# Linear attention layer of an encoder trunk: projections dealt out between decay levels, v and r in one pass of 512 columns

## The chip, the cores and the metric

The kernel runs on one core of a Trainium2 chip. The time is that of the whole program in microseconds; of several runs the median counts. The engines are TensorE (PE; its weight loads are listed apart as PEld), VectorE (DVE), ScalarE (ACT), GpSimd (POOL) and SyncE (SP), which issues the transfers. Each works through its own list of instructions in order, and semaphores hold an instruction until what it needs is there.

## What is computed

A trunk of two layers over 512 tokens of width 1024, float32: a gated DeltaNet layer, then a gated linear attention (GLA) layer, each followed by a residual LayerNorm, a squared-ReLU MLP and another LayerNorm. The change lies in the GLA layer:

```python
proj = jnp.matmul(h, w_in)                      # 512 x 1024 by 1024 x 3104
q = heads(proj[..., :B_KW], B_DK) * (B_DK ** -0.5)      # 4 heads x 128
k = heads(proj[..., B_KW:2 * B_KW], B_DK)               # 4 heads x 128
v = heads(proj[..., 2 * B_KW:2 * B_KW + B_VW], B_DV)    # 4 heads x 256
r = proj[..., 2 * B_KW + B_VW:2 * B_KW + 2 * B_VW]      # 4 heads x 256
gate_logit = einsum(gl, gate_w2) + gate_b               # gl: two directions of rank 16
log_a = log_sigmoid(gate_logit) / 16
# one direction: S_t = diag(a_t) S_{t-1} + k_t v_t^T,  o_t = S_t^T q_t
o = o_f + o_b                                           # forward and backward
o = _rmsnorm(o, norm_g) * jax.nn.silu(r)
return jnp.matmul(o, w_out)
x = _layernorm(alpha * x + m, ln1_g, ln1_b)
```

## The kernel before

Large products are split in three: each float32 operand is cut into a high part (a cast on ACT, line 74) and a low part (a subtraction on DVE, line 75), and `mm3` (lines 93 to 95) adds high by high, high by low and low by high. A weight block comes by transfer into a buffer `wst` (three of them) and is split into a pair `wh`, `wl` (three pairs), 128 x 1024 numbers each. The activations stand transposed as `xth`, `xtl`.

The GLA layer (`gla`, line 465) goes head by head. `project` makes the two gate logits `lg`, from which ACT and DVE make the decay factors `a` (forward and backward), then q and k (48 products of 512 columns together), then v and r, each in 96 products of 256 columns into two accumulator banks. Silu of r needs another function table, which is loaded and put back. POOL multiplies the result `sr` by the norm's factor.

`mix` builds the 128 x 128 scores inside a block of tokens by doubling: seven levels s = 1, 2, 4 .. 64. In a level, DVE multiplies q (`qh`, lines 607 and 608) and k (`kh`, lines 611 and 612) half by half with running products of the decays, PE makes four score products `scp` (line 596), and DVE copies the part that the level's mask names into `sc` (line 621). Then the running products double: `SF` and `PB` on POOL (lines 628, 629), the two tiles `a` on DVE (lines 630, 631). After the levels come two sets of transposes `kdp`, six state products `stp`, and for each of four token blocks the output products `op`. `finish` normalises (a reciprocal root by ACT and DVE), multiplies by `sr` (line 686), transposes (`otp`) and splits into `oth`, `otl`.

The Python code writes head h's `mix`, then head h+1's `project`, then head h's `finish`. A scheduler in the language's tile layer then orders each engine's instructions by its own estimates; nothing in the kernel pins the order of PE. During the last head's `mix`, `out_part` makes the output product over the six 128-row parts of heads 0 to 2 (`oa`); `out_last` adds the residual through a product with the identity, the two parts of head 3 (`ob`) and the LayerNorm. Accumulator banks: `pj` 2, `ac` 4, `tp` 2.

Of the kernel before, what the change touches and what calls it, by code (L numbers as in the profile page):

```python
# [8 lines left out]
F32 = mybir.dt.float32  # L9
# [19 lines left out]
class Ctx:  # L29
# [17 lines left out]
    def exp_ln_after(self, ins):  # L47

        with self.tc.issue_after(ins.ins):
            self.nc.scalar.preload_act_table_set("natural_log_exp_and_others")  # L50

# [147 lines left out]
    def out_last(self, w, ks, lhs, z, tags, par):  # L199

        nc = self.nc
        ws = [[self.wrows(w, k * P, hf * 512) for k in ks[::2]] for hf in range(2)]
        for t in range(NT):
# [11 lines left out]
            self.xpose(t, self.xt[t])  # L215
# [235 lines left out]
class GlaConst:  # L451


    def __init__(self, c, pool, gate_b, norm_g, tmp):
        nc = c.nc
        self.masks = sel_masks(c, pool, tmp)
        self.gb = pool.tile([P, 2, B_H], F32, name="gb", bufs=1)
        nc.gpsimd.dma_start(self.gb, gate_b.rearrange("n (h p) -> p n h", p=P), allow_slow_non_contiguous=True)
        self.ngb = pool.tile([P, 2, B_H], F32, name="ngb", bufs=1)
        nc.gpsimd.tensor_scalar(self.ngb, self.gb, -1.0, None, ALU.mult)  # L460
        self.gbc = pool.tile([P, B_DV], F32, name="gbc", bufs=1)
        nc.gpsimd.dma_start(self.gbc, norm_g.partition_broadcast(P))


def gla(c, gc, w_in, gate_w2, w_out, ln_g, ln_b):
    tc, nc = c.tc, c.nc
    H = B_H
    with c.banks(pj=2, ac=4, tp=2), tc.tile_pool(name="gla", bufs=2) as pool:
# [26 lines left out]
        g = (glh, gll, w2h, w2l, gc.gb, gc.ngb, gc.gbc)  # L495
# [15 lines left out]

def gla_vr(c, pool, w_in, c0, name):

    parts = []
    for q in range(2):
        st = c.wst.tile([P, 4, B_DV], F32, name="wst", tag="wst")
        c.dma(st, w_in[q * 512:(q + 1) * 512, c0:c0 + B_DV].rearrange("(k p) n -> p k n", p=P))
        parts.append(c.split(st, [P, 4, B_DV]))
    out = []
    for tp in range(2):  # L520
        ps = c.bank([P, 2, B_DV], F32, name=name, tag="pj")
        for ti in range(2):
            sl = slice((2 * tp + ti) * P, (2 * tp + ti + 1) * P)
            for k in range(KT):
                wh, wl = parts[k // 4]
                c.mm3(ps[:, ti, :], c.xth[:, k, sl], c.xtl[:, k, sl], wh[:, k % 4, :], wl[:, k % 4, :],
                      k == 0, k == KT - 1)
        out.append(ps)
    return out


class GlaHead:


    def __init__(self, c, pool, h, w_in, gates, masks, oth, otl):
        self.c, self.pool, self.h, self.w_in = c, pool, h, w_in
        self.gates, self.masks, self.oth, self.otl = gates, masks, oth, otl
# [4 lines left out]
    def project(self, qk=None):  # L542
        c, pool, h, w_in = self.c, self.pool, self.h, self.w_in
        V, A = c.nc.vector, c.nc.scalar
        H = B_H
        glh, gll, w2h, w2l, gb, ngb, gbc = self.gates

        self.A = []
        for d in range(2):
            ps = c.bank([P, S], F32, name="lg", tag="ac")  # L550
            rows = slice(32 * d, 32 * d + 16)
            c.mm3(ps, w2h[rows, h * P:(h + 1) * P], w2l[rows, h * P:(h + 1) * P], glh[rows, :], gll[rows, :], True, True)
            e = self.t2("ge", 1)
            A.activation(e, ps, AF.Abs, bias=gb[:, d, h:h + 1])
            A.activation(e, e, AF.Exp, scale=-1.0)
            A.activation(e, e, AF.Ln, bias=1.0)
            r = self.t2("gr", 1)
            A.activation(r, ps, AF.Relu, bias=ngb[:, d, h:h + 1], scale=-1.0)
            V.tensor_tensor(r, r, e, ALU.add)
            a = self.t2(f"a{d}")  # L560
            A.activation(a, r, AF.Exp, scale=-1.0 / 16.0)
            self.A.append(a)
        qps = qk[0] if qk else c.proj_cm(w_in, h * P, "pj", name="pjq")
        self.q = self.t2("q")
        A.mul(self.q, qps, float(P) ** -0.5)
        kps = qk[1] if qk else c.proj_cm(w_in, H * P + h * P, "pj", name="pjk")
        self.k = self.t2("k")
        A.copy(self.k, kps)
        self.v = pool.tile([P, NT, B_DV], F32, name="v", tag="v", bufs=2)
        for i, ps in enumerate(gla_vr(c, pool, w_in, 2 * H * P + h * B_DV, "pjv")):  # L570
            A.copy(self.v[:, 2 * i:2 * i + 2, :], ps)
        self.sr = sr = pool.tile([P, NT, B_DV], F32, name="sr", tag="sr", bufs=2)
        for i, ps in enumerate(gla_vr(c, pool, w_in, 2 * H * P + H * B_DV + h * B_DV, "pjr")):
            last = A.activation(sr[:, 2 * i:2 * i + 2, :], ps, AF.Silu)
        c.exp_ln_after(last)
        c.nc.gpsimd.tensor_tensor(sr, sr, gbc.unsqueeze(1).to_broadcast([P, NT, B_DV]), ALU.mult)

    def mix(self):
        c, pool, q, k, v = self.c, self.pool, self.q, self.k, self.v
        V, A, T, G = c.nc.vector, c.nc.scalar, c.nc.tensor, c.nc.gpsimd  # L580
        t2 = self.t2

        PF, SB = self.A
        SF, PB = t2("SF", 1), t2("PB", 1)
        c.nc.gpsimd.memset(SF, 1.0)
        c.nc.gpsimd.memset(PB, 1.0)
        sc = pool.tile([P, NT, P], F32, name="sc", tag="sc", bufs=1)

        def blk(t, s):
            return t.rearrange("p (b two s) -> p b two s", two=2, s=s)  # L590

# [10 lines left out]
        k2 = t2("kh")  # L602
        A.mul(k2, k, 2.0)
        s = 1
        while s < P:
            qh = t2("qh")
            V.tensor_tensor(blk(qh, s)[:, :, 1, :], blk(q, s)[:, :, 1, :], blk(PF, s)[:, :, 1, :], ALU.mult)  # L607
            V.tensor_tensor(blk(qh, s)[:, :, 0, :], blk(q, s)[:, :, 0, :], blk(SB, s)[:, :, 0, :], ALU.mult)
            if s > 1:
                kh = t2("kh")  # L610
                V.tensor_tensor(blk(kh, s)[:, :, 0, :], blk(k, s)[:, :, 0, :], blk(SF, s)[:, :, 0, :], ALU.mult)
                V.tensor_tensor(blk(kh, s)[:, :, 1, :], blk(k, s)[:, :, 1, :], blk(PB, s)[:, :, 1, :], ALU.mult)  # L612
            else:
                kh = k
            ps = score(kh, qh)
# [6 lines left out]

            nb = S // (2 * s)

            def bc(t, half, idx):
                return blk(t, s)[:, :, half, idx:idx + 1].to_broadcast([P, nb, s])

            G.tensor_tensor(blk(SF, s)[:, :, 0, :], blk(SF, s)[:, :, 0, :], bc(PF, 1, s - 1), ALU.mult)
            G.tensor_tensor(blk(PB, s)[:, :, 1, :], blk(PB, s)[:, :, 1, :], bc(SB, 0, 0), ALU.mult)
# [623 lines left out]
```

## Time and profile before

| | us |
|---|---|
| median of 3 runs | 1469.55 |
| the runs | 1468.07 to 1469.78 |
| the profiled execution | 1473.26 |
| its span in the profile | 1471.6 |
| PE busy | 1388.9 (94%) |
| DVE busy | 1024.1 (70%) |
| ACT busy | 682.5 (46%) |
| POOL busy | 208.6 (14%) |

The GLA layer lies at about 815 to 1130 us of the span: first projections from 815.6, the heads to 1103, then the output product. The mean granted clock of PE over the span is 0.989 of full speed. A record of a product lasts longer than the step to the next one, since products overlap in the array; steps are therefore read from starts. A row of a timeline gives start, length, engine, line, operation, out<-in, shape and count, and in brackets the idle time of the engine before it and what ended it. One float32 product shows as two records, a split one (`mm3`) as one record for each of its three.

### The profile page before, as it was taken

The numbers are of one execution on the slowest core, as the hardware profiler recorded it, in microseconds if no ns is written. First come the engines' busy times: TensorE is split into PE (matmuls) and PEld (weight loads), VectorE is DVE, ScalarE is ACT, GpSimd is POOL, SyncE is SP. The second block draws the span as 40 slices with busy tenths as digits, with TensorE's granted clock in tenths as the row PEclk, the third lists the DMA queues.
The fourth block names the chain that finished last, engine by engine and source line by source line (L and its number), as shares of the span: only waits on it lengthen the run. The fifth ranks groups of instructions, "written<-read, shape, count | busy, mean of one in ns | idle before, by whom it ended". The sixth has DMA issues, their size and how long they took to land.

```text
span 1471.6 us, 21001 instructions
## 1 busy us (share of the span) xinstructions
PE 1388.9 (94%) x8333; PEld 1141.9 (78%) x8333; DVE 1024.1 (70%) x1637; ACT 682.5 (46%) x1218; POOL 208.6 (14%) x220
## 2 busy tenths in 40 slices
PE   7999999999989999999999989899799999999997
PEld 6676777677767888888887878787677888888886
DVE  6878887988677666758655465857648577767655
ACT  3766556655633545444541434344123544454530
POOL 4221331133211300000001131222202000000000
PEclk9999999999999999999999999999899999999999
DMA  6221211211132743341121412111113642332221
GB/s 175 61 58 35 53 30 44 58 44 44 44 108 65 230 126 93 99 129 45 56 91 28 117 57 58 46 56 44 43 58 106 211 138 77 115 100 58 57 72 57
DMA packets 145882, 117.24 MB, mean 80 GB/s; under 512 B 7360, under 2 KB 122168, under 8 KB 145784
## 3 DMA queue, kind: packets, MB, share of 16 engines
q1 hardware_dynamic: 143856, 111.49, 25.8%
q0 software_dynamic: 1360, 4.33, 1.0%
q8 instruction: 65, 1.06, 0.3%
q14 instruction: 34, 0.27, 0.1%
q10 hardware_dynamic: 567, 0.08, 0.0%
HBM read 113.79 MB, written 2.10 MB: 79 GB/s over the span
## 4 chain that ended last, share of the span: by engine, by line
PE 52%; issue 27%; DVE 12%; ACT 5%; POOL 3%; DMA 2%; DVEq 0%; POOLq 0%; ACTq 0%
PE pj L93 4%; PE pj L95 4%; PE pj L94 4%; PE op L1190 2%; DVE qh L607 1%; PE pX L93 1%; PE pX L95 1%; PE pX L94 1%; POOL xt L178 1%; DVE wl L75 1%; PE pl L95 1%; PE pl L93 1%; PE oa L94 1%; PE m L1168 1%; PE pl L94 1%
## 5 line engine op out<-in xcount | busy, mean ns | idle before, releaser
L75 DVE TENSOR_TENSOR wl<-wst,wh 128x1024 fp32r<-128x1024 f32 x140 | 178.2, 1276 | 195.2 <-ACT wh L74 193.6
L74 ACT CAST wh<-wst 128x1024 fp32r<-128x1024 f32 x140 | 146.9, 1049 | 270.4 <-PE pj L94 159.3
L93 PE MATMUL pj<-xth,wh 128*128 128x512 f32 (+1 forms) x544 | 202.8, 373 | 0.7 <-ACT xth L133 0.7
L95 PE MATMUL pj<-xth,wl 128*128 128x512 f32 (+1 forms) x544 | 202.4, 372 | 1.0 <-DVE wl L75 1.0
L94 PE MATMUL pj<-xtl,wh 128*128 128x512 f32 (+1 forms) x544 | 202.3, 372 | 0.1
L75 DVE TENSOR_TENSOR w2l<-w2r,w2h 128x1024 fp32r<-128x1024 f32 x84 | 102.6, 1221 | 50.3 <-ACT w2h L74 49.9
L95 PEld LDWEIGHTS pj<-xth,wl 128*128 128x128 f32 x544 | 103.1, 190 | 19.5 <-DVE wl L75 1.5
L93 PEld LDWEIGHTS pj<-xth,wh 128*128 128x128 f32 x544 | 103.1, 190 | 18.3 <-ACT xth L133 0.9
L94 PEld LDWEIGHTS pj<-xtl,wh 128*128 128x128 f32 x544 | 103.2, 190 | 18.1 <-DVE xtl L134 0.3
L74 ACT CAST w2h<-w2r 128x1024 fp32r<-128x1024 f32 x84 | 88.2, 1050 | 58.4 <-DMA w2r<-in_mlp_w 21.1
L1044 POOL TENSOR_TENSOR off<-ath,off 128x1024 f16<-128x1024 f16 x32 | 72.5, 2274 | 40.8 <-PE lv L1086 39.4
L74 ACT CAST ah<-h 128x1024 fp32r<-128x1024 f32 x40 | 42.2, 1054 | 56.2 <-DVE h L317 21.9
L178 POOL TENSOR_TENSOR xt<-xt,ln 128x512 f32<-128x512 f32 x8 | 10.6, 1320 | 383.3 <-ACT xt L177 371.6
L1039 POOL TENSOR_TENSOR atl<-on,ath 128x512 f16<-128x512 f32 x16 | 22.2, 1392 | 243.4 <-ACT ath L1038 243.1
L94 PE MATMUL pX<-w2l,ah 128*128 128x512 f32 x144 | 56.1, 389 | 0.0
L95 PE MATMUL pX<-w2h,al 128*128 128x512 f32 x144 | 56.0, 389 | 0.0
L93 PE MATMUL pX<-w2h,ah 128*128 128x512 f32 x144 | 56.0, 389 | 0.0
L75 DVE TENSOR_TENSOR al<-h,ah 128x1024 fp32r<-128x1024 f32 x40 | 48.8, 1220 | 2.8 <-ACT ah L74 1.5
L596 PE MATMUL scp<-qh,kh 128*128 128x128 f32 x192 | 27.8, 290 | 19.1 <-DVE kh L612 19.1
L144 ACT ACTIVATE rsy<-rsv 128x1 f32<-128x1 f32 (+1 forms) x28 | 5.8, 207 | 84.9 <-DVE rsv L143 84.7
L596 PEld LDWEIGHTS scp<-qh,kh 128*128 128x128 f32 x192 | 24.1, 197 | 26.5 <-issue 20.4
L93 PE MATMUL pjk<-xth,wh 128*128 128x512 f32 (+1 forms) x112 | 42.6, 380 | 0.5 <-ACT wh L74 0.5
(446 smaller groups left out, 3827.2 us busy)
## 6 DMA issues: line engine op xcount, KB each, us to landing
wst<-in_mlp_w SPq DMA_DIRECT2D x80, 512.0 KB, 4.1
w2r<-in_mlp_w SPq DMA_DIRECT2D x48, 512.0 KB, 3.7
wst<-in_a_w_in SPq DMA_DIRECT2D x32, 512.0 KB, 4.0
wst<-in_b_w_in SPq DMA_DIRECT2D x24, 512.0 KB, 3.9
wst<-in_a_w_out SPq DMA_DIRECT2D x8, 512.0 KB, 3.7
wst<-in_b_w_out SPq DMA_DIRECT2D x8, 512.0 KB, 3.9
xt<-in_x SPq DMA_DIRECT2D x4, 512.0 KB, 7.0
z<-in_x SPq DMA_DIRECT2D x8, 256.0 KB, 5.3
```

Source lines behind the costliest of these rows:

```text
L74: nc.scalar.copy(hi, src)
L75: nc.vector.tensor_tensor(lo, src, hi.bitcast(F32), ALU.subtract)
L93: mm(ps, ah, bh, start=start, stop=False, **kw)
L94: mm(ps, ah, bl, start=False, stop=False, **kw)
L95: mm(ps, al, bh, start=False, stop=stop, **kw)
L178: nc.gpsimd.tensor_tensor(out[q], out[q], par[2 + q], ALU.add)
L596: T.matmul(ps[:, n, :], kh[:, sl], qh[:, sl], start=True, stop=True)
L607: V.tensor_tensor(blk(qh, s)[:, :, 1, :], blk(q, s)[:, :, 1, :], blk(PF, s)[:, :, 1, :], ALU.mult)
L1039: G.tensor_tensor(atl[:, us, :], at, ath[:, us, :], ALU.subtract)
L1044: eng.tensor_tensor(t, ath, m.unsqueeze(1).to_broadcast([P, U, P]), ALU.mult)
L1168: T.matmul(m2, self.xf[:, d * NT + n, :], r, start=True, stop=True)
L1190: T.matmul(op[:, n, :], l, r, start=i == 0, stop=i == len(mm) - 1)
```

## The change

- `in_order`: a block in which each PE instruction is made to follow the one written before it. The GLA heads stand in such a block, so PE's order is the order of the Python code.
- A generator `stream` yields projections in pieces of six products of 512 columns: 16 pieces for a head's v and r, 8 for the next head's q and k, and after head 3, 16 pieces of `out_pieces` over the first four parts. `behind(n)` takes n pieces. They are placed between levels (4 before s = 4, then 3 before each score) and one by one between the state and output products.
- `vr` makes v and r side by side: a weight block holds two of the eight row parts with 256 columns of v and 256 of r (two transfers), and four banks, one for each token tile, gather 512 columns each.
- Forward and backward decays stand in one tile `F`, the products that POOL kept in one tile `E`. `diag` is an access pattern that takes alternate stretches of s columns from the two halves, so that `qh`, `kh` and the doubling of `F` are one DVE instruction each over 512 columns. The doubling of `E` is two DVE instructions of 256 columns; POOL keeps one memset a head.
- The scores of s = 1 and s = 2 of the next head are placed in the output products of this one, its gates behind the levels s = 16 and 32, the norm of a head behind the pieces of level s = 8 of the next.
- The norm's factor is a column `gcol`, applied where the transposed output is copied and split.
- `out_last` now covers four parts (heads 2 and 3), and three of its four weight pairs are split into the places of `v`, `sr` and `F`. Banks: `ac` 2, `tp` 2, `pj` 4.

```diff
-    with c.banks(pj=2, ac=4, tp=2), tc.tile_pool(name="gla", bufs=2) as pool:
+    with c.banks(ac=2, tp=2, pj=4), tc.tile_pool(name="gla", bufs=2) as pool:
...
-        heads[0].project(qk0)
-        for h in range(H):
-            heads[h].mix()
-            if h + 1 < H:
-                heads[h + 1].project()
-            else:
-                for hf in range(2):
-                    c.out_part(w_out, list(range(2 * h)), lhs, z, "pj", hf)
-            heads[h].finish()
+        early = list(range(KT // 2))
+        with c.in_order(mybir.EngineType.PE):
+            list(heads[0].qk(qk0))
+            heads[0].gates(0)
+            heads[0].gates(1)
+            def stream():
+                for h in range(H):
+                    yield from heads[h].vr()
+                    yield from heads[h + 1].qk() if h + 1 < H else c.out_pieces(w_out, early, lhs, z, "pj")
...
+            behind(8)
+            after = None
+            level = heads[0].levels()
+            next(level)
+            for h in range(H):
+                for s in level:
+                    behind(0 if s == 2 else 4 if s == 4 else 3)
+                    if s == 8 and after:
+                        after()
+                    if s in (16, 32) and h + 1 < H:
+                        heads[h + 1].gates(s // 32)
+                level = heads[h + 1].levels() if h + 1 < H else iter(())
+                heads[h].states(behind, level)
+                after = heads[h].norm
+            behind(2)
+            after()
+            behind(99)
         c.new_x()
-        c.out_last(w_out, [2 * H - 2, 2 * H - 1], lhs, z, ("ac",), par)
+        c.out_last(w_out, list(range(KT // 2, KT)), lhs, z, ("pj",), par,
+                   [None, (pool, "v", "sr", 2), (pool, "F", "F", 2), (pool, "v", "sr", 2)])
...
+        for q in range(KT // 2):
+            st = c.wst.tile([P, 2, 2 * B_DV], F32, name="wst", tag="wst")
+            rows = slice(2 * q * P, 2 * (q + 1) * P)
+            for i, c0 in enumerate((v0, r0)):
+                c.dma(st[:, :, i * B_DV:(i + 1) * B_DV], self.w_in[rows, c0:c0 + B_DV].rearrange("(k p) n -> p k n", p=P))
+            wh, wl = c.split(st, [P, 2, 2 * B_DV])
+            if ps is None:
+                ps = [c.bank([P, 2 * B_DV], F32, name="pjv", tag="pj") for _ in range(NT)]
+            for t in range(NT):
...
+                yield
...
-            V.tensor_tensor(blk(qh, s)[:, :, 1, :], blk(q, s)[:, :, 1, :], blk(PF, s)[:, :, 1, :], ALU.mult)
-            V.tensor_tensor(blk(qh, s)[:, :, 0, :], blk(q, s)[:, :, 0, :], blk(SB, s)[:, :, 0, :], ALU.mult)
+            V.tensor_tensor(blk(qh, s), blk(q, s), diag(F, s), ALU.mult)
             if s > 1:
                 kh = t2("kh")
-                V.tensor_tensor(blk(kh, s)[:, :, 0, :], blk(k, s)[:, :, 0, :], blk(SF, s)[:, :, 0, :], ALU.mult)
-                V.tensor_tensor(blk(kh, s)[:, :, 1, :], blk(k, s)[:, :, 1, :], blk(PB, s)[:, :, 1, :], ALU.mult)
+                V.tensor_tensor(blk(kh, s), blk(k, s), diag(E, s), ALU.mult)
...
-            G.tensor_tensor(blk(SF, s)[:, :, 0, :], blk(SF, s)[:, :, 0, :], bc(PF, 1, s - 1), ALU.mult)
-            G.tensor_tensor(blk(PB, s)[:, :, 1, :], blk(PB, s)[:, :, 1, :], bc(SB, 0, 0), ALU.mult)
-            V.tensor_tensor(blk(PF, s)[:, :, 1, :], blk(PF, s)[:, :, 1, :], bc(PF, 0, s - 1), ALU.mult)
-            V.tensor_tensor(blk(SB, s)[:, :, 0, :], blk(SB, s)[:, :, 0, :], bc(SB, 1, 0), ALU.mult)
+            for i in range(2):
+                e = blk(E[:, i, :], s)[:, :, i, :]
+                V.tensor_tensor(e, e, bc(1 - i, 1 - i, (1 - i) * (s - 1)), ALU.mult)
+            a = F[:, 0, :]
+            x = bass.AP(a.tensor, a.offset + s, [list(a.ap[0]), [2 * s, nb], [S - 1, 2], [0, s]])
+            V.tensor_tensor(diag(F, s), diag(F, s), x, ALU.mult)
+            yield s
```

How the instructions move is seen in each engine's list. First DVE inside the levels of a middle head, around the copy of level s = 16 (`mu_6389` is its mask). Before:

```order
L607 TENSOR_TENSOR qh<-q,a_9738 128x8x32
L621 COPY_PREDICATED sc<-mu_6389,scp 128x512
L608 TENSOR_TENSOR qh<-q,a_9751 128x8x32
L612 TENSOR_TENSOR kh<-k,PB 128x8x32
L630 TENSOR_TENSOR a_9738<-a_9738 128x8x32
L611 TENSOR_TENSOR kh<-k,SF 128x4x64
L631 TENSOR_TENSOR a_9751<-a_9751 128x8x32
```

Now:

```order
L703 TENSOR_TENSOR E<-E,F 128x8x32 x2
L706 TENSOR_TENSOR F<-F 128x8x2x32
L91 TENSOR_TENSOR wl<-wst,wh 128x1024
L714 COPY_PREDICATED sc<-mu_6389,scp 128x512
L689 TENSOR_TENSOR qh<-q,F 128x512
L692 TENSOR_TENSOR kh<-k,E 128x512
```

The halves have become whole instructions, the two updates that stood on POOL stand on DVE, and splits of weights lie between the levels.

Second PE, from the transposes and first scores of a middle head to its next scores. Before (between the rows shown lie further products of `pjq`):

```order
L95 MATMUL pjr<-wh,xtl 128x256
L690 MATMUL otp<-ident,o 128x128 x8
L596 MATMUL scp<-qh,k 128x128 x4
L596 MATMUL scp<-q,kh 128x128 x4
L596 MATMUL scp<-qh,kh 128x128 x4
L93 MATMUL pjq<-xth,wh 128x512
L94 MATMUL pjq<-xtl,wh 128x512
```

Now, at the same levels, from the last output product of the head before (between the rows shown lie further products of `pjv`; the first run of them is 24 long, the second 18):

```order
L766 MATMUL op<-st_9158,qd 128x256
L678 MATMUL scp<-qh,kh 128x128 x4
L109 MATMUL pjv<-wh,xth 128x512
L110 MATMUL pjv<-wl,xth 128x512
L111 MATMUL pjv<-wh,xtl 128x512
```

```order
L785 MATMUL otp<-ident,o 128x128 x8
L678 MATMUL scp<-qh,kh 128x128 x4
L109 MATMUL pjv<-wh,xth 128x512
```

The scores that stood in a row of three, with runs of about ten q and k products behind them, now have runs of 18 to 24 products of v, r, q or k between them, and the first two levels have moved up into the head before.

Third PE at the end of the last head. Before, 118 `oa` products lie between the last output product and the transposes:

```order
L673 MATMUL op<-st_10765,kh 128x256
L94 MATMUL oa<-wl,oth 128x512
L95 MATMUL oa<-wh,otl 128x512
L93 MATMUL oa<-wh,oth 128x512
```

Now it is the last `out_pieces`, the output product, and 14 `ob` products (two with the identity, twelve of `mm3`):

```order
L766 MATMUL op<-st_10446,qd 128x256
L241 MATMUL ob<-xt_5720,ident 128x512
L109 MATMUL ob<-wh,oth 128x512
L110 MATMUL ob<-wl,oth 128x512
L111 MATMUL ob<-wh,otl 128x512
```

and on ACT beside it, where `v<-wst` is the cast of the last weight block into the place of `v`:

```order
L768 COPY o<-op 128x256
L90 CAST v<-wst 128x1024
L770 ACTIVATE sq,ss<-o 128x256
L160 ACTIVATE rsy<-rsv 128x4
L161 ACTIVATE rsy<-rsy 128x4
L788 ACTIVATE oth<-otp,gcol 128x512 x2
```

The stream is used up there, so the norm of the last head has the first products of `out_last` beside it, and the cast stands ahead of the last sum of squares.

More of the change, by code (lines that the diff above doesn't have):

```diff
@@ L50, in exp_ln_after, with in_order @@
             self.nc.scalar.preload_act_table_set("natural_log_exp_and_others")
+    @contextlib.contextmanager
+    def in_order(self, engine):
+        traced = self.nc.cur_bb.bb.instructions
+        last = traced[-1]
+        yield
+        start = next(k for k in reversed(range(len(traced))) if traced[k] is last) + 1
+        prev = None
+        for i in list(traced[start:]):
+            if i.engine == engine:
+                if prev is not None:
+                    self.tc.add_manual_dep(
+                        i, prev.name, mybir.DependencyInfo(mybir.DependencyClass.NoSync, mybir.DependencyReason.DATA),
+                        reason="in_order")
+                prev = i
     @contextlib.contextmanager
@@ L539, in t2, with gates @@
     def t2(self, name, bufs=2):
         return self.pool.tile([P, S], F32, name=name, tag=name, bufs=bufs)
-    def project(self, qk=None):
-        c, pool, h, w_in = self.c, self.pool, self.h, self.w_in
+    def gates(self, d):
+        c, h = self.c, self.h
         V, A = c.nc.vector, c.nc.scalar
[L545 to L568, printed above, removed]
-        self.v = pool.tile([P, NT, B_DV], F32, name="v", tag="v", bufs=2)
[L570 to L576, printed above, removed]
@@ new lines, in gates, with qk @@
+        V.tensor_tensor(r, r, e, ALU.add)
+        A.activation(self.F[:, 1 - d, :], r, AF.Exp, scale=-1.0 / 16.0)
+    def qk(self, ps=None):
+        c, h = self.c, self.h
+        A = c.nc.scalar
+        self.q, self.k = self.t2("q"), self.t2("k")
+        for i, (t, nm) in enumerate(((self.q, "pjq"), (self.k, "pjk"))):
+            if ps is None:
+                wh, wl = c.wcols(self.w_in, (i * B_H + h) * P)
+                bk = c.bank([P, S], F32, name=nm, tag="pj")
+                for k in range(KT):
+                    c.mm3(bk, wh[:, k, :], wl[:, k, :], c.xth[:, k, :], c.xtl[:, k, :], k == 0, k == KT - 1)
+                    if k % 2:
+                        if k == KT - 1:
+                            self.keep(i, t, bk)
+                        yield
+            else:
+                self.keep(i, t, ps[i])
@@ L639, in kdec @@
             for n in range(NT):
[L640 to L641 removed]
+                T.transpose(ps[:, n, :], kd[d][:, n * P:(n + 1) * P], c.ident)
+            o = pool.tile([P, NT, P], F32, name=f"kdt{d}", tag=f"kdt{d}", bufs=1)
             A.copy(o, ps)
[L643 to L653 removed]
+            kt.append(o)
@@ L654, in mix @@
+        states = [{}, {}]
+        cur = [None, None]
+        for i in range(NT - 1):
+            for d in range(2):
+                if i < 2 and d == 0:
+                    behind(1)
+                n = i if d == 0 else NT - 1 - i
+                ps = c.bank([P, B_DV], F32, name="stp", tag=("ac", "tp")[d])
+                T.matmul(ps, kt[d][:, n, :], v[:, n, :], start=True, stop=True)
                 nw = pool.tile([P, B_DV], F32, name=f"st{d}", tag=f"st{d}", bufs=3)
-                if cur is None:
+                if cur[d] is None:
@@ L669, in mix @@
+                    V.scalar_tensor_tensor(nw, cur[d], tot, ps, ALU.mult, ALU.add)
+                states[d][n + 1 - 2 * d] = cur[d] = nw
+        self.ss = c.small.tile([P, NT], F32, name="ss", tag="ss")
+        self.ob = {}
+        for n in (1, 2, 0, 3):
+            behind(1)
+            if n != 1 and n != 3:
+                next(level, None)
             sl = slice(n * P, (n + 1) * P)
-            ops = c.bank([P, B_DV], F32, name="op", tag="ac")
+            ops = c.bank([P, B_DV], F32, name="op", tag=("ac", "tp")[n % 2])
```

169 lines of the change are left out of this document (101 added, 68 removed).

## Prediction

> **What bounds the kernel now.** I read the stage first: the busy time of each engine between the head of the linear attention layer and its output product (columns: length; busy time and instructions of PE, PEld, DVE, ACT, POOL; clock; DMA share).
>
> ```profile
> 833.00:1105.00 272.00, 246.19 (x1576) 216.96 (x1574) 174.61 (x309) 105.50 (x191) 59.00 (x66) 0.97 0.19 55
> ```
>
> TensorE (PE) is the busiest, VectorE (DVE) is at 64%, nothing else is near. Then who made PE wait there (total, times, longest):
>
> ```profile
> PE scp L596 <- DVE kh L612: 19.1, 20, 2.4
> PE pjr L94 <- DVE wl L75: 4.9, 4, 2.3
> PE stp L653 <- ACT kdt L642: 1.4, 2, 0.7
> ```
>
> The scores `scp` wait for `kh`, the last DVE product of a decay level. The PE timeline shows how one level looks, and the same score one head later (988.72):
>
> ```profile
> 929.57 0.39 PE L94 MATMUL pjq<-xtl,wh 128*128 128x512 f32 x1
> 930.90 1.16 PE L596 MATMUL scp<-qh,kh 128*128 128x128 f32 x8 [0.94 <-DVE kh L612]
> 931.81 0.47 PE L95 MATMUL pjq<-xth,wl 128*128 128x512 f32 x1
> ...
> 933.51 0.40 PE L93 MATMUL pjq<-xth,wh 128*128 128x512 f32 x1
> 934.62 1.13 PE L596 MATMUL scp<-qh,kh 128*128 128x128 f32 x8 [0.71 <-DVE kh L612]
> ...
> 988.72 1.16 PE L596 MATMUL scp<-qh,kh 128*128 128x128 f32 x8 [0.94 <-DVE kh L612]
> ```
>
> A level lasts 3.7 us (930.90 to 934.62), of which PE has 0.9 us of score and 1.9 us of `pjq`. A head lasts 57.8 us. The level is 3.7 us long because DVE and POOL go in turn:
>
> ```profile
> 878.99 0.85 DVE L607 TENSOR_TENSOR qh<-q,a 128x256 f32<-128x256 f32 x1
> ...
> 880.38 0.41 DVE L608 TENSOR_TENSOR qh<-q,a 128x256 f32<-128x256 f32 x1
> ...
> 881.37 0.85 DVE L611 TENSOR_TENSOR kh<-k,SF 128x256 f32<-128x256 f32 x1
> ...
> 882.48 0.84 DVE L607 TENSOR_TENSOR qh<-q,a 128x256 f32<-128x256 f32 x1
> ```
>
> ```profile
> 878.88 0.68 POOL L628 TENSOR_TENSOR SF<-SF,a 128x256 f32<-128x256 f32 x1 [0.76 <-DVE kh L611]
> 881.26 0.68 POOL L629 TENSOR_TENSOR PB<-PB,a 128x256 f32<-128x256 f32 x1 [1.70 <-DVE kh L612]
> ```
>
> The same 128x256 product takes 0.41 us alone and 0.85 when it starts under a POOL product. So the level sections run at the pace of DVE and PE is half filled, while v and r, 192 products a head, run in one dense block in which DVE has little to do.
>
> **What PE's work is without waits.** Rows for the step from one product to the next:
>
> ```profile
> 839.26 0.38 PE L93 MATMUL pjv<-wh,xth 128*128 128x256 f32 x1
> 839.48 0.28 PE L94 MATMUL pjv<-wl,xth 128*128 128x256 f32 x1
> 850.76 0.28 PE L95 MATMUL pjv<-wh,xtl 128*128 128x256 f32 x1
> 927.49 0.40 PE L94 MATMUL pjq<-xtl,wh 128*128 128x512 f32 x1
> 1039.77 0.60 PE L690 MATMUL otp<-ident,o 128*128 128x128 f32 x4
> 1040.21 1.06 PE L596 MATMUL scp<-qh,k 128*128 128x128 f32 x8
> 1041.10 1.06 PE L596 MATMUL scp<-q,kh 128*128 128x128 f32 x8
> 1075.48 0.59 PE L673 MATMUL op<-v,sc 128*128 128x256 f32 x2
> 1075.91 0.59 PE L673 MATMUL op<-st,kh 128*128 128x256 f32 x2
> 1104.32 1.02 PE L208 MATMUL ob<-xt,ident 128*128 128x512 f32 x2
> ```
>
> From 839.48 to 850.76 lie 94 steps of 256 columns: 0.120 us each. From 927.49 to 929.57 lie nine of 512 columns: 0.231. Eight score records take 0.89, so 0.111 each; two `op` records 0.43; four transposes 0.44. Between the first v product (839.26) and the output product (1104.32) lie 265.1 us. The work in it: v and r 768 x 0.120 = 92.2; q and k of three heads 144 x 0.231 = 33.3; `oa` 144 x 0.231 = 33.3; scores 256 x 0.111 = 28.4; `op` 80 and `stp` 48 x 0.215 = 27.5; transposes 64 x 0.11 = 7.0; gate products of three heads, 18 at 0.231 at most, 4.2. Sum 225.9, so **39 us are lost**. The waits above name 25; each is shown some 0.16 short, since a 0.39 record lasts past its 0.23 step. Most of the rest is slow clock, as behind the wait for `wl` (same columns as the first row):
>
> ```profile
> 909.00:912.00 3.00, 0.91 (x8) 0.70 (x6) 2.24 (x5) 2.21 (x2) 1.01 (x1) 1.00 0.00 0
> 912.00:915.00 3.00, 2.83 (x13) 2.83 (x14) 1.25 (x2) 0.00 (x0) 0.00 (x0) 0.52 0.55 148
> ```
>
> **The change part by part.**
>
> *The stream between levels.* Each head's 24 pieces of six 512-column products (6 x 0.231 = 1.39 us) are now dealt out: 4, then 3 per level, then one by one between the state products. A level then holds 3 x 1.39 + 0.89 = 5.1 us of PE work against DVE's. DVE per head, from the groups of the stage (count, busy, mean ns):
>
> ```profile
> L75 DVE TENSOR_TENSOR wl<-wst,wh 128x1024 fp32r<-128x1024 f32 x30 | 36.7, 1236 | 54.7 <-ACT wh L74 54.4
> L621 DVE COPY_PREDICATED sc<-mu,scp 128x512 f32<-128x512 uint8 x24 | 17.3, 720 | 0.5 <-PE scp L596 0.5
> L608 DVE TENSOR_TENSOR qh<-q,a 128x256 f32<-128x256 f32 x28 | 11.5, 412 | 1.2 <-ACT a L561 1.1
> L686 DVE SCALAR_TENSOR_TENSOR o<-o,rs,sr 128x256 f32<-128x256 f32 x16 | 8.5, 590 | 0.1
> L658 DVE SCALAR_TENSOR_TENSOR st<-st,a,stp 128x256 f32<-128x256 f32 x16 | 7.6, 477 | 4.0 <-PE stp L653 3.9
> L664 DVE TENSOR_TENSOR kh<-q,a 128x512 f32<-128x512 f32 x8 | 5.1, 680 | 0.0
> ```
>
> Six `wl` 7.4; 26 products of 512 (`qh` 7, `kh` 6, `F` 7, `kd` 2, `qd` 2, `gr` 2) at 0.68, 17.7; 14 updates of `E`, new on DVE, at 0.412, 5.8; 7 masked copies 5.0; 4 states 1.9; 4 `o` 2.4; two `otl` taken as 512-column products 1.4; the small ones of the root 0.8. Sum **42.4 us**. PE in a middle head has v and r 22.2 (below), q and k 11.1, and a quarter of the other terms, (28.4 + 27.5 + 7.0)/4 = 15.7, with gates about 50 us. So PE becomes the bound of the whole head, with DVE at 85%, and no POOL product is left to hold DVE up. For a level: 0.68 x 3 + 0.41 x 2 + 0.72 = 3.6 us and a `wl` in most, 4.8 at most against 5.1.
>
> What I walked through in the order lists for one middle head: `kh` and `qh` stand one to two levels ahead of their score; the copies `kdt` have a piece between them and `stp`; each score bank is read a piece or more before it comes round again. The tight places are the second score right behind the first eight (its bank waits for ACT's copy `sc`), and casts `wh` that stand in ACT's queue ahead of such copies. Bounds of the remaining waits: 0 to 5 us a head (today's 39 us are about 10 a head, and a cast is a quarter of that). I take 1.5 a head, near the lower end, since nothing in the walk was late: **+6** with **-39** for what goes.
>
> *v and r together.* 384 products of 512 columns instead of 768 of 256: 384 x 0.231 = 88.7, **-3.5** (0.009 us for each pair made one).
> The Trainium skill ("TensorE: Matmul & The Clock Gate", "Wait — 56ns, not 53.3ns?") puts a product's step at its columns over 2.4 GHz and about 2.5 ns. By it a pair made one saves 2.5 ns, an estimate of 1.0 us in all; the rows above differ, and I go by them. Silu and its table loads stay, four halves instead of two wholes, on ACT with 105.5 busy of 272. The multiplication of `sr` on POOL goes; the factor enters in two existing instructions.
>
> *The junction before it.*
>
> ```profile
> 815.63 0.29 PE L93 MATMUL gps<-xth,wh 128*48 128x256 f32 x1 [0.87 <-DVE xt L282]
> 819.33 0.66 PE L130 MATMUL tp<-ident,xt 128*128 128x128 f32 x4 [0.78 <-DVE xt L175]
> 820.64 0.66 PE L130 MATMUL tp<-ident,xt 128*128 128x128 f32 x4 [0.66 <-POOL xt L178]
> ```
>
> PE's list now has 30 q and k products (3.6 us) ahead of these transposes instead of 24 gate ones (2.7), and 18 behind them, where PE waited for `xth`. The first and third wait stay (they hang on the last residual add and on POOL), the second and the ones behind go, about 1.8, and a stretch of half clock that followed: **-3**, bounds 0 and -5.
>
> *The tail.* The last head's norm has nothing left in the stream. Today 118 `oa` products (27 us) stand between the last `op` and its transposes; laid bare it costs its whole chain, from the last `op` (1075.91) to the end of the four `o` products:
>
> ```profile
> 1079.64 1.67 DVE L686 SCALAR_TENSOR_TENSOR o<-o,rs,sr 128x256 f32<-128x256 f32 x4
> ```
>
> ```profile
> L74 ACT CAST wh<-wst 128x1024 fp32r<-128x1024 f32 x31 | 32.6, 1052 | 77.6 <-PE pjq L94 26.9 <-PE oa L95 20.3 <-PE pjr L95 14.9
> ```
>
> 1081.3 - 1076.2 = 5.1 us, of which some 1.2 are two additions of `oa` that won't lie there; a cast (1.05), new on ACT ahead of the last `sq`, makes it 5. PE has 14 `ob` products ahead of the transposes: two with the identity, a pair of records and about 0.9 each (1104.32), and twelve of 0.231, 4.6 us. Left open 0.4, then `oth`, the split of the last weights and `otl` one behind the other under the second identity product, about 1 more: **+1.5**, bounds 0 and +5. The upper one is the whole chain open and a half clock behind it, as the rows at 909 show one after 3 us with 0.9 us of work.
> The Trainium skill ("TensorE: Matmul & The Clock Gate", "What's actually happening") lets the clock fall after an idle window of about 3.4 us. The stretch at 909 was not idle throughout and fell all the same, so the looser reading by the row stays in the bound; by the page the upper end would be +4.
>
> **Sum**: -39 + 6 - 3.5 - 3 + 1.5 = -38. Against the profiled execution (1473.26, span 1471.6), from whose rows it is made, that is 1435.3. That execution stands 3.7 us over the median of the runs, 1469.55, so in their terms it is **1432 us** (1431.6).
>
> **Rivals.**
> *Order too stiff.* PE's order is now fixed, so whatever is late blocks all behind it. Casts (1.05 us) wait until PE has used up the block three before (the weights have three buffers), and they stand ahead of `kdt`, `sc` and `o` in ACT's queue. Four such hits a head: 4 x 4 x 1.05 = 17 instead of 6, and the tail at +5: 1432 + 11 + 3 = 1446. For it: `wl` and casts are what PE waited for at 909. Against: the old block needed two v parts at once until all v was done; now a part is free after 5.6 us.
> *Nothing left open*: no remaining wait, tail 0, junction -5: 1432 - 6 - 1.5 - 2 = 1422.
> *Slower: DVE takes over.* The 20 products a head that reach across both halves of `F` or `E` have no row before. Taken at 0.68 they leave DVE at 42.4; at (57.8 - 42.4)/20 = 0.77 more, 1.45 us each, DVE is as long as today's head, and above that the kernel is slower. At 1.7: 42.4 + 20.4 = 62.8, +5 a head, 1490 us. Against it: `L608`, whose runs go from one element in two up to 64, has mean 412 ns over all 28.
> The Trainium skill ("SBUF — State Buffer", "Door 1: The DMA port swizzle") says an access that crosses to a new 16-byte line pays; no row shows such a jump at each element. By it only the two products at s = 1 would pay, not 20.
> *It does little*: gains eaten by waits nobody sees, 1469.
>
> **How the numbers follow.** Forecast 0.68 (1423 to 1441), stiff order 0.18, nothing open 0.07, slower 0.05, little 0.02. The range 1420 to 1451 leaves out the two last cases, the worse half of the stiff one and a little below. Faster by over 0.2% (about what a measurement of this kernel can tell from no change) 0.93, same 0.02, slower 0.05.
>
> **What would show it.** Right: scores with waits under 0.3 us, next to no half clock between the heads, PE products of v and r at 0.231, DVE near 85% and POOL empty there, a head of 51 to 53 us. Wrong: two-half products over 1 us; PE waiting for ACT copies in the states; a tail gap over 5 us.

## The result, and the profile after

The changed kernel takes 1429.46 us (median of 4 runs, 1427.94 to 1431.42) against 1468.93 us for the kernel before (4 runs, the same chip): a ratio of 0.9732, 95% interval 0.9715 to 0.9749, 39.5 us faster. The forecast was 1432 us, in a range of 1420 to 1451. The profiled execution took 1431.42 us; its span is 1429.7.

First the view that carried the forecast: the busy time of each engine in a stretch of time (columns as in the prediction), for the changed kernel. The first row is the heads from their first levels to the output product, the second 50 us in the middle of them.

```profile
838.00:1050.00 212.00, 212.00 (x1082) 177.68 (x1080) 160.09 (x274) 105.86 (x196) 2.86 (x3) 1.00 0.22 68
940.00:990.00 50.00, 50.00 (x259) 41.86 (x258) 37.49 (x65) 26.51 (x50) 0.95 (x1) 1.00 0.20 64
```

PE is busy for the whole of it, at full clock, where it had 246 of 272 us at a clock of 0.97. POOL has gone from 59.0 us to 2.9. DVE is at 75%.

Second, what PE waited for, from the heads to the end of the output product's LayerNorm (total, times, longest):

```profile
PE tp L146 <- POOL xt L194: 1.8, 4, 0.6
PE otp L785 <- DVE o L781: 0.3, 1, 0.3
PE pj L110 <- DVE xtl L150: 0.3, 1, 0.3
```

All of these lie behind 1050; up to there no wait of PE is listed. The 19.1 us for `kh` and the 4.9 for `wl` are gone.

Third, PE's timeline over one head, transposes to transposes (start, length, engine, line, operation, out<-in, shape, count):

```profile
931.62 0.60 PE L736 MATMUL kdp<-ident,ge 128*128 128x128 f32 x4
...
950.94 1.05 PE L678 MATMUL scp<-qh,kh 128*128 128x128 f32 x8
...
957.33 1.05 PE L678 MATMUL scp<-qh,kh 128*128 128x128 f32 x8
...
963.19 1.06 PE L678 MATMUL scp<-qh,kh 128*128 128x128 f32 x8
...
969.17 1.16 PE L678 MATMUL scp<-qh,kh 128*128 128x128 f32 x8
...
982.66 0.60 PE L736 MATMUL kdp<-ident,ge 128*128 128x128 f32 x4
```

A head lasts 51.0 us (982.66 - 931.62) where it lasted 57.8, and no score has a bracket with a wait. The scores shown are 5.9 to 6.4 us apart (the last two of the head, 975.26 and 980.39, 5.1), longer than the 3.7 before, since a level now holds the work that stood in the dense block.

Fourth, the borders by which the gain can be put in its places, on PE:

```profile
815.68 0.39 PE L111 MATMUL pl<-w2r 128*128 128x512 f32 x1
...
836.84 0.50 PE L109 MATMUL pjv<-wh,xth 128*128 128x512 f32 x1
837.17 0.39 PE L110 MATMUL pjv<-wl,xth 128*128 128x512 f32 x1
...
840.16 0.39 PE L111 MATMUL pjv<-wh,xtl 128*128 128x512 f32 x1
...
1049.46 1.02 PE L241 MATMUL ob<-xt,ident 128*128 128x512 f32 x2
```

`pl` is the last product of the MLP ahead of the layer. In the kernel before it stands here:

```profile
814.37 0.39 PE L95 MATMUL pl<-w2r 128*128 128x512 f32 x1
```

| stretch | before | after | difference |
|---|---|---|---|
| last `pl` to first v product | 24.9 | 21.2 | -3.7 |
| first v product to output product | 265.1 | 212.6 | -52.4 |
| output product to the end of the span | 367.2 | 380.2 | +13.0 |
| last `pl` to the end | 657.2 | 614.0 | -43.2 |

48 products of `oa` (two of six parts; 48 x 0.231 = 11.1 us) have moved from the second stretch into the third. Without this move the second is -41.4 and the third +1.9. The spans differ by only 41.9, because the unchanged work ahead of `pl` took 1.3 us longer in this execution. That stretch varies: over the ten profiles of this study in which nothing ahead of `pl` was edited, the last `pl` starts at 811.6 to 815.7. So below, profiles are compared from the last `pl` to the end, and this number is called **the rest**: 657.2 before, 614.0 now.

### The profile page after: what moved, and what is told of

Its sections match the earlier page's. It is cut to its first block, busy times and chain, and to the rows that moved or that the text cites. A ratio compares the mean times of both kernels' runs of the same rounds, so it can differ in the third digit from the quotient of the medians.

```text
span 1429.7 us, 20124 instructions
## 1 busy us (share of the span) xinstructions
PE 1373.9 (96%) x7949; PEld 1117.8 (78%) x7949; DVE 1017.0 (71%) x1613; ACT 689.9 (48%) x1234; POOL 153.6 (11%) x156
## 4 chain that ended last, share of the span: by engine, by line
PE 58%; issue 28%; DVE 6%; ACT 5%; POOL 2%; DMA 1%; DVEq 0%; POOLq 0%; ACTq 0%
PE pj L110 4%; PE pj L111 4%; PE pj L109 4%; PE pjv L109 3%; PE pjv L111 2%; PE pjv L110 2%; PE scp L678 2%; PE op L1285 2%; PE pjq L111 1%; PE pjq L109 1%; PE pjq L110 1%; PE pjk L111 1%; PE pjk L110 1%; PE pjk L109 1%; PE op L766 1%
## 5 line engine op out<-in xcount | busy, mean ns | idle before, releaser
L91 DVE TENSOR_TENSOR wl<-wst,wh 128x1024 fp32r<-128x1024 f32 x137 | 175.2, 1280 | 163.8 <-ACT wh L90 162.5
L90 ACT CAST wh<-wst 128x1024 fp32r<-128x1024 f32 x137 | 143.6, 1048 | 240.3 <-PE pj L110 166.9
L111 PEld LDWEIGHTS pj<-xth,wl 128*128 128x128 f32 x544 | 102.9, 189 | 19.1 <-DVE wl L91 1.3
L109 PE MATMUL pjv<-wh,xth 128*128 128x512 f32 x128 | 54.8, 428 | 0.0
L111 PE MATMUL pjv<-wh,xtl 128*128 128x512 f32 x128 | 50.2, 392 | 0.0
L110 PE MATMUL pjv<-wl,xth 128*128 128x512 f32 x128 | 49.9, 390 | 0.0
```

The costliest lines, as they stand in the source:

```text
L90: nc.scalar.copy(hi, src)
L91: nc.vector.tensor_tensor(lo, src, hi.bitcast(F32), ALU.subtract)
L109: mm(ps, ah, bh, start=start, stop=False, **kw)
L110: mm(ps, ah, bl, start=False, stop=False, **kw)
L111: mm(ps, al, bh, start=False, stop=stop, **kw)
```

## The experiments

Two theories stood against each other. The first says that the gain comes from the order: with projections behind each score, PE has work while DVE makes the next level. The second says that it comes from the cheaper level on DVE and from the end of the turns with POOL. One more kernel sizes a single term, two look for the point at which DVE takes over, two try what the new profile suggests. No experiment changes the outputs; the extra products in two of them are written to a tile and replaced at once. The runs below were taken in three sets on three chips, each with the kernel before beside it (medians 1470.60, 1469.21 and 1470.01 us): the ratios are against these, and a difference of a microsecond between medians of two sets says little. In the diffs, line by line, - is the kernel that the edit starts from.

### v and r in 256 columns again

```diff
-                    c.mm3(ps[t], c.xth[:, k, sl], c.xtl[:, k, sl], wh[:, j, :], wl[:, j, :], k == 0, k == KT - 1)
+                    for n in range(2):
+                        cs = slice(n * B_DV, (n + 1) * B_DV)
+                        c.mm3(ps[t][:, cs], c.xth[:, k, sl], c.xtl[:, k, sl], wh[:, j, cs], wl[:, j, cs],
+                              k == 0 and n == 0, k == KT - 1, skip_group_check=True)
```

> The changed kernel with v and r again in products of 256 columns (768 instead of 384), all else kept, the order of the pieces too. By the rows before (0.120 us for 256 columns, 0.231 for 512) 768 x 0.120 - 384 x 0.231 = +3.5 us, so 1433.0 us against 1429.5. If the wide pass were worth nothing, since PE has other slack, 1429.5. If the step of a product were its columns over 2.4 GHz and 2.5 ns, +1.0: 1430.5.

It took 1433.87 us (ratio 0.9748, 0.9733 to 0.9762). Two kernels timed beside it on the same chip, which behave as the change does (next section), took 1429.50 and 1429.74, so the price is 4.1 to 4.4 us. The rest of its span is 617.9, 3.9 more. Its PE timeline has the step of a 256-column product:

```profile
842.74 0.28 PE L109 MATMUL pjv<-wh,xth 128*128 128x256 f32 x1
...
843.94 0.28 PE L110 MATMUL pjv<-wl,xth 128*128 128x256 f32 x1
```

Ten steps in 1.20 us: 0.120 each, and in the change thirteen of 512 columns from 837.17 to 840.16, 0.230 each. 384 x (0.240 - 0.230) = 3.8 us. With PE full, all of it shows in the time.

### The old level body in the new order

Once whole (the products by halves on DVE, the doubling of `E` on POOL), and once only the doubling of `E` on POOL:

```diff
-            V.tensor_tensor(blk(qh, s), blk(q, s), diag(F, s), ALU.mult)
+            for i in (1, 0):
+                V.tensor_tensor(blk(qh, s)[:, :, i, :], blk(q, s)[:, :, i, :], blk(F[:, i, :], s)[:, :, i, :], ALU.mult)
...
-                V.tensor_tensor(e, e, bc(1 - i, 1 - i, (1 - i) * (s - 1)), ALU.mult)
+                c.nc.gpsimd.tensor_tensor(e, e, bc(1 - i, 1 - i, (1 - i) * (s - 1)), ALU.mult)
```

> The changed kernel with the level body of before: products of q and k half by half, the doubling of E on POOL, that of F in two DVE instructions. Theory 1 (the gain comes from dealing the projections out between the levels, so that DVE's level time is hidden): a level of 3.7 us and a split of weights of 1.2 still fit under 5.1 to 6 us of PE, so 0 to +5: 1429 to 1435. Theory 2 (the gain comes from the cheaper level on DVE and the end of the turns with POOL): most of the gain is gone, over 1450.

> The changed kernel with the doubling of E on POOL instead of DVE, the wide products of q, k and F kept. It puts back the turns between DVE and POOL alone. Theory 1: hidden, 0 to +3, 1429 to 1433. Theory 2: a level gets 2 x 0.7 us longer, 7 x 1.4 x 4 = 39 us in the worst case, about 1460.

They took 1429.74 (0.9723, 0.9706 to 0.9739) and 1429.50 us (0.9723, 0.9706 to 0.9740), with a rest of 614.6 and 614.3: no difference from the change. The middle of the heads with the old body:

```profile
940.00:990.00 50.00, 50.00 (x259) 41.83 (x258) 37.71 (x74) 26.48 (x50) 13.46 (x15) 1.00 0.21 64
```

POOL is back with 13.5 us, DVE has as many busy microseconds as in the change (37.7 against 37.5), and PE is full all the same. The groups of DVE in that kernel's heads show that the turns with POOL are back as well:

```profile
L708 DVE TENSOR_TENSOR F<-F 128x256 f32<-128x256 f32 x56 | 31.6, 586 | 11.0 <-POOL E L705 10.9
```

DVE waits 10.9 us for POOL before these updates, and one of them takes 586 ns. PE shows of it one wait of 0.5 us for `qh`; the rest is hidden. The second theory falls for this order: here the body is worth nothing that these runs can tell.

### The stream in lumps

Everything as in the change, but v and r in one block, q and k between the levels, nothing between the state products:

```diff
-            behind(8)
+            behind(16)
...
-                    behind(0 if s == 2 else 4 if s == 4 else 3)
+                    behind({2: 0, 4: 2, 8: 2, 16: 2, 32: 1, 64: 1}[s])
...
-                heads[h].states(behind, level)
+                heads[h].states(lambda n: None, level)
+                behind(16)
```

> The changed kernel with the stream taken in lumps, as before: v and r of the next head in one block of 16 pieces behind the outputs, q and k (8 pieces) between the levels, nothing between the state products. DVE's new level body, the 512-column pass and the pinned order stay. Theory 1: levels bare again, about 3.4 us of DVE against 2.6 of PE, a head of about 55.5 instead of 51.0 us: +18, 1447, between 1440 and 1460. Theory 2: the level body carries the gain, 1429 to 1435.

It took 1449.41 us (0.9854, 0.9839 to 0.9869); the rest is 636.2, 22.1 more than in the change. Its waits of PE, over heads and output product:

```profile
PE kdp L737 <- DVE ge L726: 9.6, 4, 2.7
PE scp L679 <- DVE qh L690: 1.7, 1, 1.7
PE scp L679 <- DVE kh L693: 1.3, 1, 1.3
PE scp L679 <- ACT sc L712: 0.9, 1, 0.9
```

and the engines while the levels of a middle head run:

```profile
912.00:932.00 20.00, 18.77 (x105) 15.15 (x103) 19.09 (x32) 11.87 (x18) 0.00 (x0) 1.00 0.19 54
```

DVE is at 95% there and PE no longer full: the wait has moved from the scores to the transposes behind the last level. Half of the gain of the change is gone by the order alone, with the new body in place. The first theory's 1447 was near. The waits listed come to 13.5 of the 22.1 us. Most of the others is slow clock behind the waits, as in the last head:

```profile
1040.00:1046.00 6.00, 3.13 (x20) 2.36 (x18) 6.00 (x13) 2.09 (x2) 0.00 (x0) 0.96 0.25 87
1046.00:1052.00 6.00, 5.28 (x16) 4.25 (x17) 4.05 (x7) 1.92 (x4) 0.00 (x0) 0.50 0.15 38
```

Over the 232 us from 838 to 1070 the granted clock is 0.96, where the change has 1.00. By these two figures up to 232 x 0.04 = 9 us are lost to the clock, an estimate.

What the pin does by itself is not shown: every kernel with the stream was run with it. What this experiment changes is the order in which the pieces are written.

### The new level body in the kernel before

```diff
-            V.tensor_tensor(blk(qh, s)[:, :, 1, :], blk(q, s)[:, :, 1, :], blk(PF, s)[:, :, 1, :], ALU.mult)
-            V.tensor_tensor(blk(qh, s)[:, :, 0, :], blk(q, s)[:, :, 0, :], blk(SB, s)[:, :, 0, :], ALU.mult)
+            V.tensor_tensor(blk(qh, s), blk(q, s), diag(F, s), ALU.mult)
```

and likewise `kh`, `E` and `F` as in the change; no stream, no written order.

> The kernel before with the new level body alone (F and E in one tile each, wide products, no POOL in a level); projections, banks, norm and output product as before. The scheduler's list for it is not that of before: it now places 13 to 28 products behind each score of levels 4 to 64 where it placed about 10, since it sees cheaper levels, and v products move there too. Theory 1 (what counts is how much PE work lies behind a level): most of the waits for kh go by this order, -25 to -35, 1440. Theory 2 (the shorter level itself): 0.4 us in 24 levels, -10, 1459, with waits of 0.5 us left at the scores.

It took 1442.15 us (0.9816, 0.9798 to 0.9834), 27 us less than the kernel before. That is near the first theory's 1440. So the body that is worth nothing in the new order goes with most of the gain in the old one. Its wait for the scores:

```profile
PE scp L599 <- DVE kh L613: 4.3, 4, 1.6
```

4.3 us where the kernel before has 19.1. But this is not the body alone: with other instructions the scheduler made another list for PE, in which most scores from s = 4 on have 12 to 28 products behind them. What is left of the wait follows that list. The four waits stand at the scores of s = 4, which have none, 7, 9 and 7 products ahead of them in the four heads; no score with 12 or more ahead of it has a wait. In the second head, 7 products lie between the first two rows and 13 between the last two:

```profile
917.47 1.06 PE L599 MATMUL scp<-qh,kh 128*128 128x128 f32 x8
...
921.09 1.16 PE L599 MATMUL scp<-qh,kh 128*128 128x128 f32 x8 [0.96 <-DVE kh L613]
...
925.08 1.05 PE L599 MATMUL scp<-qh,kh 128*128 128x128 f32 x8
```

### Lumps and the old body together

This holds PE's order fixed while the body goes back: the two edits above in one kernel.

> Lumps and the old level body together: the fourth corner beside the change (new order, new body, 1429.5), the new order with the old body (1429.7) and lumps with the new body (1449.4). Theory 1, read as 'the order alone matters': about 1450, as the body was worth nothing under the new order. Theory 1 read as 'whichever of PE and DVE is longer sets a level': in lumps a level has 2.3 to 3.7 us of PE work, so DVE and POOL show through; the old body's level took 3.5 to 3.7 us plus the split of a weight, the new one's 3.4 us with most splits: 0.5 to 1 us more in each of 20 levels, so 1459 to 1469, with waits for kh and qh of 10 us and more in all. It also says whether the 27 us that the new body saved on the kernel before came from the body or from the scheduler's other order.

It took 1456.86 us (0.9908, 0.9885 to 0.9931), 7.4 more than lumps with the new body (the two are of different sets; by the ratios it is 7.9); the rest is 641.9, 5.7 more. The waits and the engines over the levels of a middle head:

```profile
PE kdp L739 <- DVE ge L728: 15.1, 4, 4.6
PE scp L679 <- DVE kh L695: 2.6, 2, 1.6
```

```profile
915.00:936.00 21.00, 19.71 (x111) 15.77 (x109) 18.84 (x37) 11.25 (x18) 6.53 (x8) 1.00 0.18 51
```

The body counts where DVE sets the pace of the levels, but with 6 to 8 us for 28 levels, 0.2 to 0.3 us each, it counts less than the 0.5 to 1 that I expected, and most of the wait stands at the transposes (15.1 us), not at the scores where I expected it. It follows that the order is worth some 20 us with the new body (1449.4 to 1429.5) and 27 with the old one (1456.9 to 1429.7), and the body about 7 or nothing. What share of the 27 us in the kernel before came from the scheduler's other list was not measured with that list held fixed; by this comparison the body alone would not explain it. Nor are the lumps the kernel before again: lumps with the old body are still some 13 us faster than it, by the rest 15.3. Of these the junction (3.7) and the pass of 512 columns (3.9) explain half; the remainder was not put in its places.

### How much more DVE could carry

Two, and then four, more products of 512 columns in each level:

```diff
+            for _ in range(2):
+                V.tensor_tensor(qh, q, F[:, 0, :], ALU.mult)
             V.tensor_tensor(blk(qh, s), blk(q, s), diag(F, s), ALU.mult)
```

> The changed kernel with two more DVE products of 512 columns in each of the 28 levels (written into qh and overwritten at once). 14 a head at some 0.62 us a step = 8.7 us. In a middle head of the changed kernel DVE is busy 37.5 of 50 us, so 12.5 are free. If the room in DVE is a sum over the head: 0 to +3, 1429 to 1433. If each level's own chain counts (3.3 + 1.2 for a split + 1.2 = 5.7 us against 5.1 to 6 of PE): about half a microsecond in 5 levels of 4 heads, +10, 1440. If DVE were the bound: 4 x 8.7 = +35, 1464.

> Four more products in each level, 17.4 us a head against 12.5 free. By the sum over the head DVE is 4.9 us a head too long: +15 to +20, 1447. By the chain of each level (6.9 us against 5.1 to 6): about 1.4 us in 6 levels of 4 heads, +34, 1463. No change would mean that the copies and splits counted as DVE time can wait longer than thought.

With two it took 1435.01 us (0.9764, 0.9747 to 0.9780), with four 1467.44 (0.9986, 0.9977 to 0.9995). The middle of the heads, first with two:

```profile
935.00:985.00 50.00, 50.00 (x259) 41.92 (x258) 45.04 (x81) 25.58 (x49) 0.96 (x1) 1.00 0.22 64
```

then with four, and below that its first wait:

```profile
935.00:985.00 50.00, 45.72 (x236) 38.05 (x235) 49.39 (x89) 21.73 (x44) 0.95 (x1) 1.00 0.20 60
```

```profile
PE scp L678 <- DVE qh L691: 20.3, 10, 5.2
```

With DVE at 90% PE is still full, and the middle heads last 51.1 and 51.0 us as in the change. Of the 5.5 us that the two products cost, the waits name 4.8: two for `qh` at the start of the first head's levels, where DVE is busy 9.97 of 10 us (850 to 860), and one for `wl` in the last head.

```profile
847.00 1.16 PE L678 MATMUL scp<-qh,k 128*128 128x128 f32 x8 [0.65 <-DVE qh L691]
...
851.16 1.13 PE L678 MATMUL scp<-qh,kh 128*128 128x128 f32 x8 [2.11 <-DVE qh L691]
...
1036.12 0.50 PE L110 MATMUL oa<-wl,oth 128*128 128x512 f32 x1 [1.98 <-DVE wl L91]
```

With four products DVE is at 99% and PE waits for it: the whole gain is gone. Neither expectation was right in both cases: with two products the time lies between the two, nearer to the sum of a head's work, and the middle heads show no wait at all; with four it is nearer to the chain of the levels.

### The halves of the LayerNorm that POOL makes

The waits left in the new profile are `tp <- POOL xt`: the second half of a LayerNorm's scaling goes through ACT and POOL (line 194). Moved to DVE, first in the LayerNorm behind the output products (of both layers, which share the code), then in all:

```diff
-            self.layernorm(pss, self.xh(t), par)
+            self.layernorm(pss, self.xh(t), par, last=True)
```

```diff
-            if last or q == 0:
+            if True:
```

> The changed kernel with the LayerNorm of the attention output made on DVE alone: its second half is no longer scaled by ACT and added to by POOL (0.72 and 1.26 us and two waits), but one DVE product of 0.74. The second transpose of each tile waits for POOL 0.4 to 0.76 us in the changed kernel, 2.5 us over four tiles. Expected -1 to -2.5: 1427 to 1428.5. If DVE is the bound of that stretch (busy 34 of 51 us): 0 or slower.

> All four LayerNorms wholly on DVE, where e7 moved those behind the two output products. In e7's profile PE still waits 2.5 us, 4 times, for the POOL half in the LayerNorms behind the two MLPs. If these waits go and DVE's copy comes as soon: 1.5 to 2.5 less than e7, 1421.5 to 1422.5. If DVE itself is late there, the waits change their name and the time stays at 1424.

The first took 1423.90 us (0.9690, 0.9674 to 0.9707), the second 1420.51 (0.9660, 0.9639 to 0.9681): both faster than the kernel before and than the change. For the first, the rest is 611.9, 2.2 us less than in the change; by the medians it is 5.6 less in all, so some 3 us would lie ahead of the last `pl`, where the same edit changes the first layer's LayerNorm. The trace bears this out with a border of its own, the first product of the first layer's output (`ob`):

```profile
437.26 1.02 PE L241 MATMUL ob<-z,ident 128*128 128x512 f32 x2
...
808.56 0.39 PE L111 MATMUL pl<-w2r 128*128 128x512 f32 x1
```

From there to the last `pl` are 371.3 us, and 373.8 to 375.2 in the ten profiles named above. I had priced the waits that the profile names; the change has these between 800 us and the end:

```profile
PE tp L146 <- POOL xt L194: 3.1, 6, 0.7
```

The first kernel has 1.2 us of them left, 1.9 less, near the 2.2. In the second kernel none is left there, and no wait on DVE took its place. Its step of 3.4 us from the first is larger than expected, but the two are of different sets, and its runs spread over 4.1 us (1419.18 to 1423.33). In the profiles it is 2.8: 1.9 from `ob` to the last `pl` (369.4) and 0.9 in the rest (611.0).

## Why the prediction was right, point by point

**The bound.** The chain of the reading held: PE half filled between the scores, DVE and POOL in turns. The cause was the missing work behind each score; how long a level is counts only where that work is missing. The old, slower level in the new order costs nothing; the lumps bring half of the loss back. The prediction gave the stream -39 and counted no part of it for the body. Only the kernels in which the projections are not dealt out, the lumps and the kernel before, show the body's worth.

**The stream: -39 and +6.** Here the sum was off. -36.5 was forecast for the heads with v and r, -41.4 came. The work without waits is 225.9 - 3.5 - 11.1 = 211.3 us, and the stretch took 212.6: 1.3 us lost in four heads where I had put 6. I had taken 1.5 us a head because I could not show that nothing would be late; the walk through the lists, in which nothing was late, was the better evidence, and the value, 0.3 a head, lay close to the lower bound of 0.

**DVE at 85%.** It is at 75%: 42.4 us a head were forecast, and 160.09/212 of 51.0 is 38.5. The durations were right: in the groups of the head from 931.62 on, count times mean adds up to 42.8 us. But records overlap, and DVE is busy for only 38.5 of these. In DVE's timeline

```profile
959.05 0.67 DVE L689 TENSOR_TENSOR qh<-q,F 128x512 f32<-128x512 f32 x1
959.64 0.68 DVE L692 TENSOR_TENSOR kh<-k,E 128x512 f32<-128x512 f32 x1
960.25 1.22 DVE L91 TENSOR_TENSOR wl<-wst,wh 128x1024 fp32r<-128x1024 f32 x1
```

a product of 0.67 is followed after 0.59, one of 0.68 after 0.61: records overlap by some 0.08 there, and over a whole head by 42.8 - 38.5 = 4.3 us. For PE I had counted steps, for DVE lengths.

**v and r: -3.5.** 3.8 by the steps, 3.9 in the rest of the span, 4.1 to 4.4 by the runs. The rule of the Trainium skill ("TensorE: Matmul & The Clock Gate", "Wait — 56ns, not 53.3ns?"), a fixed 2.5 ns for each product, gave an estimate of 1.0 us; the trace does not agree, and the measurement decides: a pair made one saved about 10 ns here.

**The junction: -3, measured -3.7.** The third wait stayed, as forecast:

```profile
821.96 0.33 PE L146 MATMUL tp<-ident,xt 128*128 128x128 f32 x1 [0.66 <-POOL xt L194]
```

**The tail: +1.5, measured +1.9.** The gap at the transposes is there and small, as the sum of products ahead of them had it:

```profile
1053.71 0.39 PE L111 MATMUL ob<-F,otl 128*128 128x512 f32 x1
1054.40 1.07 PE L785 MATMUL otp<-ident,o 128*128 128x128 f32 x8 [0.30 <-DVE o L781]
```

The step there is 0.69 where 0.23 is normal: 0.46 lost against the 0.4 forecast. What makes up the other 1.4 us was not put in its places. The upper bound, a half clock behind a long gap, was not reached: the gap is 0.30 us, while the half clock in the lumps stands behind 6 us with 3.13 us of work.

**The rivals.** *Order too stiff*: no wait for a cast or copy of ACT shows in the heads; it fell. *Nothing left open*, 1422, was near for the heads but not for the tail or the junction. *DVE takes over* fell at its condition. The groups of DVE in the heads (busy, mean ns | idle before and what ended it):

```profile
L703 DVE TENSOR_TENSOR E<-E,F 128x256 f32<-128x256 f32 x56 | 21.2, 418 | 2.1 <-POOL E L663 1.1 <-ACT F L600 0.8
L706 DVE TENSOR_TENSOR F<-F 128x512 f32<-128x512 f32 x28 | 21.1, 754 | 0.6
L689 DVE TENSOR_TENSOR qh<-q,F 128x512 f32<-128x512 f32 x28 | 19.6, 699 | 17.7 <-PE scp L678 17.7
L692 DVE TENSOR_TENSOR kh<-k,E 128x512 f32<-128x512 f32 x24 | 16.4, 682 | 0.0
```

The products across both halves take 0.68 to 0.75 us, and DVE now waits for PE (17.7). The price named for it came close: the prediction put the point where the gain is lost at 15.4 us more DVE work a head, and four extra products in each of seven levels (28 x 0.61 = 17.1 us a head) brought the time to 0.9986 of the kernel before. That is in part luck, since the 15.4 were counted from 42.4 us a head; from the measured 38.5 the same sum gives 57.8 - 38.5 = 19.3, and less than that was enough, because the first head alone became 15.4 us longer (from the last `pl` to its transposes, 80.3 against 64.9) and the other three 5 to 9 us.

**s = 1.** The Trainium skill ("SBUF — State Buffer", "Door 1: The DMA port swizzle") lets an access pay that crosses to a new 16-byte line each time, and counts two hits on a line as enough for full bandwidth. By it only the two products at s = 1, whose elements alternate between two halves of a tile, would pay. The trace agrees. One head's DVE rows, s = 1 and then s = 2:

```profile
928.88 0.84 DVE L689 TENSOR_TENSOR qh<-q,F 128x512 f32<-128x512 f32 x1
...
931.36 1.14 DVE L706 TENSOR_TENSOR F<-F 128x512 f32<-128x512 f32 x1
...
932.95 0.66 DVE L689 TENSOR_TENSOR qh<-q,F 128x512 f32<-128x512 f32 x1
...
935.33 0.67 DVE L706 TENSOR_TENSOR F<-F 128x512 f32<-128x512 f32 x1
```

0.84 against 0.66 and 1.14 against 0.67, within 0.03 in all four heads: 0.65 us a head, hidden behind PE.

**The sum.** -3.7 - 41.4 + 1.9 = -43.2 from the last `pl` on, where -38 was forecast; 1.3 us of it went to the unchanged work ahead in this execution. In medians it is -39.5, because the profiled execution before stood further above its median (4.3 us) than the one after (2.0). So the forecast of 1432 is nearer to 1429.46 than its sum was to the trace: the sum was 5 us short, nearly all of it in the 6 us put down for waits, and 3 us of that stayed hidden: the 1.3 us ahead, and 1.7 because the forecast took off 3.7 us to get to a median and the execution after stands only 2.0 above its own. The path was right; that the number came out within 3 us is in part luck.

## What to carry to other kernels

Where one engine waits at each step of a chain on another, look first for independent work to put behind each step, and only then at the length of the step: here the order was worth 20 to 27 us and the shorter step about 7 or nothing, depending on which of the two engines was longer. Measure the room left on the hidden engine by adding work to it: two more products a level cost 5.5 us, none of it in the middle heads, and four took the whole gain. Sum an engine's work by the steps between starts, not by the lengths of records, and read the waits that remain as the list of what to do next: it gave another 9 us here.

## What the runs showed that I had not expected

- The same work ahead of the change, in kernels in which nothing there was edited, ended at 811.6 to 815.7 us in ten profiles. A difference of 3 us in the span of one execution says nothing without a border near the edit.
- A level body that loses 10.9 us to POOL's turns and one that loses 1.1 give the same median to 0.3 us when PE is full.
- From 45.0 of 50 us of DVE work to 49.4, the price went from 5.5 us to 38: the step from hidden to bound lies within 9 us of work a head.
